# A hybrid decoder step on one core: the opening rebuilt, and 1/rms applied when a product leaves PSUM

## The chip, the cores and the metric

The kernel runs on one core of one Trainium2 chip. A core has five engines that run side by side and meet at semaphores: TensorE (PE, matmuls and, as PEld, the loading of their stationary operand), VectorE (DVE), ScalarE (ACT), GpSimd (POOL) and SyncE (SP, which here only issues transfers). Matmuls read SBUF and write PSUM. The metric is the device time of one execution in microseconds. The kernel before takes 1238.84 us, the median of three runs (1238.34 to 1242.91).

## The reference

One step of a one-layer decoder over 336 rows: 16 learned meta rows, 256 prompt rows and 8 sequences of 8 new rows, each of width 2048, all in float32. Cut to what matters here:

```python
xn = rms_norm(h, norm_w)                      # x * rsqrt(mean(x*x) + eps) * norm_w
proj = xn @ w_in                              # 2048 -> z | x,B,C | dt | z_pool | u | two gates
xbc, conv_new = causal_dwconv(x_B_C, ...)     # 4 taps, then silu
y = ssd(xs, softplus(dt), B, C, state) + xs * d_skip
y = group_norm(y * silu(z)) * ssd_norm_w      # 4 groups of 512 columns
branch_ssd  = y @ w_proj_ssd
pooled = means(u, windows 2, 4, 8, 16) - u
branch_pool = (pooled @ mix + b) * scale * silu(z_pool) @ w_proj_pool
h_new = h + (sigmoid(g1) * branch_ssd + sigmoid(g2) * branch_pool) @ w_out
y_out = rms_norm(h_new, final_norm_w)
```

The norm divides a whole row of x by one number. So 1/rms may be applied to x, or to the product of the unnormed x with a weight, column by column of the transposed product.

## The kernel before, in words

Everything is held transposed: columns of the model on the 128 partitions, the 336 rows (T) along the free axis. x is 16 slices of 128 x 336, kept as four tiles of four slices, its quarters.

A **unit** is one block of 128 output columns: a product over 16 slices, for which a weight tile arrives as two halves of 128 x 1024. Matmuls take operands of type fp32r, so each operand is split into a rounded high part and a low rest, and three products are added: high x high, low x high, high x low. One unit is thus 48 matmuls into one PSUM buffer (`acc`). The weights are split as they come: ScalarE rounds (`prep_hi`, line 144), VectorE subtracts (`prep_lo`, line 150). There are 156 units in a fixed list: 4 B, 4 C, 16 xs, 16 z, then gates, the branch products, pooling and the output.

The order of the work is written out by hand. A unit has four **ticks**, one per quarter of its product. At tick `q` the program emits one step of weight preparation, one quarter of matmuls, and then whatever was put down for that tick with `at(q, ...)` or `later(d, ...)`. Each engine executes its own instructions in that order, so a tick is a place in every queue, not a time. Three halves of weights are prepared ahead of the matmuls; four buffers of each kind (`raw`, `hi`, `lo`) bound how far.

*Opening* (lines 184 to 268). Ten matmuls on ones warm TensorE up. For unit 0, each quarter of x is scaled by `norm_w` and split without its row norm (`wh`, `wl`), and its 12 matmuls follow, with four small ones for dt. Meanwhile GpSimd and ScalarE square x and GpSimd adds the squares. After unit 1 `rstd_make` turns their sum into 1/rms over all 336 rows at once. Units 0 to 7 use `wh`, `wl`; their evacuation multiplies by 1/rms (`raw=True` in `conv`). During them `xnorm` makes a second, normed split of x (`xh`, `xl`) on VectorE, ScalarE and GpSimd, which units 8 and later use; their evacuations from PSUM are ScalarE copies, Silu or Sigmoid.

*SSD stage* (ticks 52 to 152 and a little beyond). The state-space part of four groups, 24 ticks apart, is woven into the xs and z units. In it GpSimd scales the carried states (`hin`, line 624) and masks B (`bm`, line 482), TensorE makes the new states (`ps_hn`, line 630), and VectorE adds them. `z_evac` forms silu(z), multiplies y and squares it; GpSimd adds the four squares of a group (`ss`, line 667); `norm_group` sums them over the partitions with one matmul by ones (`ps_gn`, line 672).

## Time and profile before

| what | value |
|---|---|
| runs | 1238.84 us median, 1238.34 to 1242.91 |
| the profiled execution, its span | 1239.1 us, at a mean granted clock of 0.994 |
| TensorE busy | 1203.4 us (97%), 8066 instructions |
| VectorE, ScalarE, GpSimd busy | 728.4, 557.7, 159.4 us |
| HBM read and written | 186.34 and 15.32 MB |

The profile is one execution. Its views are: groups of equal instructions (busy time in all, mean of one in ns, idle time before them and what ended it), the busy time of each engine by stretch of time, the timeline (start, length, engine, line, operation, output and inputs; the bracket is the idle time before it and what ended that), and lists of who waited for whom. Matmuls are pipelined: the time of one is read from the distance between two starts, not from its own length.

### The profile page before, as it was taken

To read this page: it belongs to the slowest core of one execution; us is meant where nothing else is said; L and a number is where in the kernel's file an instruction comes from. 1 tells how busy PE (TensorE), PEld (TensorE's weight loads), DVE (VectorE), ACT (ScalarE), POOL (GpSimd) and SP (SyncE) were. 2 spreads that over 40 slices of the span, in tenths; PEclk is the share of its full clock that TensorE was granted. 3 is DMA by queue.
4 is the path that set the end of the run, shared out by engine and by line. 5 is a ranking of instruction groups with operands and counts; after the bars stand their busy time and mean duration, and the time that the engine had idled before them with its cause. 6 is when DMAs were issued, how large, how long until landed. Compare 5 with 4: busy or idle time off the path is not lost.

```text
span 1239.1 us, 19826 instructions
## 1 busy us (share of the span) xinstructions
PE 1203.4 (97%) x8066; PEld 1165.4 (94%) x8066; DVE 728.4 (59%) x1008; ACT 557.7 (45%) x792; POOL 159.4 (13%) x161
## 2 busy tenths in 40 slices
PE   6999999999999999999999999999999999999995
PEld 4988988888988999999999999999999999999995
DVE  8798789888887733433445465564343345554543
ACT  4356575748474633333334443434343333334441
POOL 7251142425344000000000000000000000000000
PEclk9999999999999999999999999999999999999998
DMA  5335637475746444444456545554444444456432
GB/s 221 125 125 182 219 126 257 146 243 170 246 143 212 152 156 151 154 153 144 150 161 174 161 150 164 156 156 153 154 153 150 144 149 154 152 170 208 151 120 85
DMA packets 82715, 202.49 MB, mean 163 GB/s; under 512 B 26512, under 2 KB 31280, under 8 KB 82608
## 3 DMA queue, kind: packets, MB, share of 16 engines
q1 hardware_dynamic: 82256, 199.58, 49.9%
q0 software_dynamic: 368, 1.65, 0.4%
q8 instruction: 63, 1.03, 0.3%
q14 instruction: 28, 0.23, 0.1%
HBM read 186.34 MB, written 15.32 MB: 163 GB/s over the span
## 4 chain that ended last, share of the span: by engine, by line
PE 83%; DVE 7%; issue 5%; POOL 3%; ACT 1%; DMA 1%; DVEq 0%; SPq 0%; POOLq 0%; ACTq 0%
PE acc L212 27%; PE acc L213 26%; PE acc L214 26%; DVE lo L150 2%; POOL hin L624 2%; DVE cacc L320 1%; DVE wl L230 1%; DVE x L282 1%; DMA raw<-wall 1%; PE ps_st L565 1%; PE ps_y L579 1%; POOL ss L667 1%; DVE hn L955 0%; POOL bm L482 0%; DVE hin L632 0%
## 5 line engine op out<-in xcount | busy, mean ns | idle before, releaser
L150 DVE TENSOR_TENSOR lo<-raw,hi 128x1024 fp32r<-128x1024 f32 x312 | 392.6, 1260 | 352.6 <-ACT hi L144 352.5
L144 ACT ACTIVATE hi<-raw 128x1024 fp32r<-128x1024 f32 x312 | 329.8, 1058 | 530.5 <-PE acc L213 438.3
L212 PE MATMUL acc<-xh,hi 128*128 128x320 f32 (+4 forms) x1536 | 480.5, 313 | 0.0
L213 PE MATMUL acc<-xl,hi 128*128 128x320 f32 (+4 forms) x1536 | 477.9, 311 | 0.0
L214 PE MATMUL acc<-xh,lo 128*128 128x320 f32 (+4 forms) x1536 | 476.9, 310 | 0.7 <-DVE lo L150 0.7
L212 PEld LDWEIGHTS acc<-xh,hi 128*128 128x128 f32 x1536 | 288.8, 188 | 2.6 <-issue 1.3
L214 PEld LDWEIGHTS acc<-xh,lo 128*128 128x128 f32 x1536 | 288.9, 188 | 1.0 <-DVE lo L150 1.0
L213 PEld LDWEIGHTS acc<-xl,hi 128*128 128x128 f32 x1536 | 288.7, 188 | 1.2
L213 PE MATMUL acc<-pl,hi 128*128 128x320 f32 x256 | 79.4, 310 | 0.0
L214 PE MATMUL acc<-ph,lo 128*128 128x320 f32 x256 | 79.3, 310 | 0.0
L212 PE MATMUL acc<-mh,hi 128*128 128x320 f32 x256 | 79.2, 309 | 0.0
L213 PE MATMUL acc<-ml,hi 128*128 128x320 f32 x256 | 79.1, 309 | 0.0
L214 PE MATMUL acc<-mh,lo 128*128 128x320 f32 x256 | 79.1, 309 | 0.0
L212 PE MATMUL acc<-ph,hi 128*128 128x320 f32 x256 | 79.1, 309 | 0.0
L212 PE MATMUL acc<-yh,hi 128*128 128x320 f32 x256 | 78.7, 308 | 0.0
L213 PE MATMUL acc<-yl,hi 128*128 128x320 f32 x256 | 78.7, 308 | 0.0
L214 PE MATMUL acc<-yh,lo 128*128 128x320 f32 x256 | 78.7, 308 | 0.0
L624 POOL TENSOR_TENSOR hin<-hin,E 128x512 f32<-128x512 f32 x32 | 50.9, 1618 | 52.4 <-ACT E L542 41.9
L320 DVE SCALAR_TENSOR_TENSOR cacc<-rawf,par,cacc 128x360 f32<-128x360 f32 (+1 forms) x72 | 49.1, 682 | 2.1 <-ACT cacc L316 0.4
L212 PEld LDWEIGHTS acc<-ph,hi 128*128 128x128 f32 x256 | 48.4, 189 | 0.0
L213 PE MATMUL acc<-wl,hi 128*128 128x336 f32 (+1 forms) x128 | 43.7, 341 | 4.8 <-DVE wl L230 4.7
L214 PEld LDWEIGHTS acc<-ph,lo 128*128 128x128 f32 x256 | 48.2, 188 | 0.0
(221 smaller groups left out, 1436.8 us busy)
## 6 DMA issues: line engine op xcount, KB each, us to landing
raw<-wall SPq DMA_DIRECT2D x312, 512.0 KB, 3.5
hin<-ssmT SPq DMA_DIRECT2D x16, 512.0 KB, 6.8
ossms<-hin SPq DMA_DIRECT2D x16, 512.0 KB, 5.8
bc<-acT SPq DMA_DIRECT2D x8, 672.0 KB, 6.9
hn<-xT SPq DMA_DIRECT2D x4, 640.0 KB, 6.9
x<-xT SPq DMA_DIRECT2D x3, 672.0 KB, 8.2
opool<-u SPq DMA_DIRECT2D x16, 100.0 KB, 3.1
oconv<-rawf SPq DMA_DIRECT2D x24, 45.5 KB, 4.0
```

What stands on the lines that cost most here:

```text
L144: S.activation(hi, r, AF.Copy)
L150: V.tensor_tensor(out=lo, in0=r, in1=hi.bitcast(F32), op=ALU.subtract)
L212: PE.matmul(acc[:, :n], lhsT=hi[:, c], rhs=bh, start=first, stop=False)
L213: PE.matmul(acc[:, :n], lhsT=hi[:, c], rhs=bl, start=False, stop=False)
L214: PE.matmul(acc[:, :n], lhsT=lo[:, c], rhs=bh, start=False, stop=last)
L230: V.scalar_tensor_tensor(out=wl[q][:, c, :], in0=xg[q][:, c, :], scalar=pc("norm_w", k), in1=wh[q][:, c, :].bitcast(F32), op0=ALU.mult, op ...
L282: V.scalar_tensor_tensor(out=x, in0=x, scalar=pc("norm_w", k), in1=rstd, op0=ALU.mult, op1=ALU.mult)
L320: V.scalar_tensor_tensor(out=a[:, a0:], in0=r[:, a0 + k:k + ACCW], scalar=pc("conv_w", 4 * c + k), in1=a[:, a0:], op0=ALU.mult, op1=ALU.add)
L565: PE.matmul(p, lhsT=st["bt"][:, i, :], rhs=st["xdt"][:, i, :], start=(i == 0), stop=False)
L579: PE.matmul(p[64 * e:64 * e + 64, a:b], lhsT=st["xdt"][:n, i, 64 * hh:64 * hh + 64], rhs=m[:n, e, o:o + b - a], start=(i == 0), stop=(i == ...
L624: GP.tensor_tensor(out=hv, in0=hv, in1=E, op=ALU.mult)
L667: later(1, lambda: GP.tensor_tensor(out=gn[g], in0=gn[g], in1=sq, op=ALU.add))
```

## The change

The opening is written anew, and the second split of x is gone.

- Units 0 and 1 go through the quarters of x together: 24 matmuls per quarter, ordered by part (high x high of both units, low x high, high x low). The half tiles of unit 1 are loaded and split in between. There are 16 warm-up matmuls for 10.
- In the opening GpSimd has no arithmetic and issues no transfers: scaling the dt weights is VectorE's, the squares are ScalarE's, their sums VectorE's (behind the fourth quarter), and `ident`, `sconv`, `umask` and `cmask` are loaded through SP.
- The unnormed split is kept for the whole kernel (its tiles now lie in the long-lived slots). So every evacuation of a product with x multiplies by 1/rms, on VectorE: `conv` always, `u_evac`, and `times_rstd` in `z_evac`, `zp_evac`, `gs_evac`, `gp_evac`, with ScalarE's Silu or Sigmoid one tick later. The copy of the conv history goes from GpSimd to ScalarE.
- `spread_rstd` replaces `rsqrt`, for x and for the four group norms: three matmuls sum over the partitions into a 128 x 3 result, the root is taken on those, VectorE makes three diagonal tiles, and three matmuls by ones spread the result over all partitions.
- The first evacuations come at ticks 14, 16, 18 and so on.

```diff
-NACC, NTR, NWARM = 3, 3, 10
+NACC, NTR, NWARM = 3, 3, 16
...
+    def spread_rstd(ss, n, scale, name, done):
+        at_ = (0, 128, n - 128)
+        p = ps.tile([128, 512], F32, tag="st", name=f"ps_sum{name}")
+        for i, t0 in enumerate(at_):
+            PE.matmul(p[:, i:i + 1], lhsT=ss[:, t0:t0 + 128], rhs=ones[:, 0:1], start=True, stop=True, skip_group_check=True)
...
+        def f1():
+            V.tensor_scalar(out=v, in0=p[:, 0:3], scalar1=scale, scalar2=EPS, op0=ALU.mult, op1=ALU.add)
+            S.activation(t, v, AF.Sqrt)
+        def f2():
+            V.reciprocal(out=r, in_=t)
...
+            for i in range(3):
+                V.tensor_scalar(out=dg[:, i, :], in0=ident, scalar1=r[:, i:i + 1], scalar2=None, op0=ALU.mult)
+        def f3():
+            q = ps.tile([128, 512], F32, tag="st", name=f"ps_rs{name}")
+            for i, t0 in enumerate(at_):
+                PE.matmul(q[:, t0:t0 + 128], lhsT=ones, rhs=dg[:, i, :], start=True, stop=True, skip_group_check=True)
+            later(1, lambda: done(q))
+        later(1, f1)
+        later(2, f2)
+        later(3, f3)
...
+    for q in range(4):
+        h = q // 2
+        if q == 0:
+            prep_hi(0, 0)
+            split_hi(0)
+            prep_hi(1, 0)
+            split_lo(0)
+            prep_lo(0, 0)
+            V.tensor_copy(out=pbs, in_=warm[:, 0:16])
+            prep_lo(1, 0)
+            V.tensor_tensor(out=wdt, in0=wdt, in1=par[:, o:o + 16].unsqueeze(2).to_broadcast([128, KT, NH]), op=ALU.mult)
         else:
+            split_hi(q)
+            if q < 3:
+                prep_hi(q - 1, 1)
+            split_lo(q)
+            if q < 3:
+                prep_lo(q - 1, 1)
+        for part in range(3):
+            for u in range(2):
...
+    prep_hi(2, 0)
+    for q in range(4):
+        S.activation(sq[q], xg[q], AF.Square)
+    prep_hi(2, 1)
+    prep_lo(2, 0)
+    for d, e in ((0, 1), (2, 3), (0, 2)):
+        V.tensor_tensor(out=sq[d], in0=sq[d], in1=sq[e], op=ALU.add)
...
-    def xnorm(k):
-        q, c = divmod(k, 4)
-        x = xg[q][:, c, :]
-        V.scalar_tensor_tensor(out=x, in0=x, scalar=pc("norm_w", k), in1=rstd, op0=ALU.mult, op1=ALU.mult)
...
-        GP.tensor_copy(out=rs[:, :, 0:3], in_=sconv[:, c, :].rearrange("p (b j) -> p b j", b=NSEQ))
+        S.activation(rs[:, :, 0:3], sconv[:, c, :].rearrange("p (b j) -> p b j", b=NSEQ), AF.Copy)
...
-        else:
-            S.activation(r[:, 3 + lo:3 + NP_], acc[:, 0:NP_ - lo], AF.Copy)
-            S.activation(rs[:, :, 3:], v(acc, lo), AF.Copy)
+        V.tensor_tensor(out=r[:, 3 + lo:3 + NP_], in0=acc[:, 0:NP_ - lo], in1=rstd[:, lo:NP_], op=ALU.mult)
+        V.tensor_tensor(out=rs[:, :, 3:], in0=v(acc, lo), in1=v(rstd, 0), op=ALU.mult)
...
+    def times_rstd(t, acc):
+        V.tensor_tensor(out=t, in0=acc[:, 0:TV], in1=rstd[:, NMETA:T], op=ALU.mult)
...
-        S.activation(sz, acc[:, 0:TV], AF.Silu)
+        times_rstd(sz, acc)
         y = xs[g][:, c, NMETA:T]
-        later(1, lambda: V.tensor_tensor(out=y, in0=y, in1=sz, op=ALU.mult))
+        later(1, lambda: S.activation(sz, sz, AF.Silu))
+        later(2, lambda: V.tensor_tensor(out=y, in0=y, in1=sz, op=ALU.mult))
...
-    at(7, rstd_make)
-    at(11, draw_turn)
-    for k in range(KT):
-        at(8 + 5 * k // 4, lambda k=k: xnorm(k))
+    now[0] = 8
+    at(9, rstd_make)
+    at(15, draw_turn)
...
-                at(max(4 * i + 4, 8 + i), lambda i=i, k=kind, j=idx, a=acc: evac(i, k, j, a))
+                at(max(4 * i + 4, 14 + 2 * i), lambda i=i, k=kind, j=idx, a=acc: evac(i, k, j, a))
```

Three places show how instructions move. First TensorE's queue at its start. Before (`acc_138` is unit 0, the numbered `wh`, `wl` the quarters, `hi_0`, `lo_0` the parts of a first half tile):

```order
L204 MATMUL ps_warm<-ones 128x128 x10
L212 MATMUL acc_138<-wh_100,hi_0_139 128x336
L213 MATMUL acc_138<-wl_104,hi_0_139 128x336
L214 MATMUL acc_138<-wh_100,lo_0_141 128x336
L212 MATMUL acc_138<-wh_100,hi_0_139 128x336
```

Now (`acc_153` is unit 0, `acc_154` unit 1; the split of x is called `xh`, `xl`):

```order
L225 MATMUL ps_warm<-ones 128x128 x16
L275 MATMUL acc_153<-xh_101,hi_0_155 128x336 x4
L275 MATMUL acc_154<-xh_101,hi_0_161 128x336 x4
L275 MATMUL acc_153<-xl_105,hi_0_155 128x336 x4
L275 MATMUL acc_154<-xl_105,hi_0_161 128x336 x4
L275 MATMUL acc_153<-xh_101,lo_0_167 128x336 x4
L275 MATMUL acc_154<-xh_101,lo_0_170 128x336 x4
L278 MATMUL ps_dt_152<-x_93,wdt 32x336 x4
```

A slice's low part stood in the second place of the queue; now eight matmuls stand ahead of the first low part of x and sixteen ahead of the first low part of a weight.

Second, GpSimd's queue around the group norm of group 0, in the SSD stage of group 2 (`ss` sums the squares `sqy`, `hin` are the carried states). Before:

```order
L482 TENSOR_TENSOR bm_1_2938<-br_2848,umask 120x640
L667 TENSOR_TENSOR ss_2701<-ss_2701,sqy_3003 128x320
L624 TENSOR_TENSOR hin_0_2811<-hin_0_2811,E_2698 128x512 x2
L667 TENSOR_TENSOR ss_2701<-ss_2701,sqy_3094 128x320
L624 TENSOR_TENSOR hin_1_2813<-hin_1_2813,E_2698 128x512 x2
```

Now, and on to the last add for group 1 (`ss_3104`):

```order
L685 TENSOR_TENSOR ss_2659<-ss_2659,sqy_2983 128x320
L638 TENSOR_TENSOR hin_0_2770<-hin_0_2770,E_2656 128x512 x2
L638 TENSOR_TENSOR hin_1_2772<-hin_1_2772,E_2656 128x512 x2
L685 TENSOR_TENSOR ss_2659<-ss_2659,sqy_3081 128x320
L638 TENSOR_TENSOR hin_2_2831<-hin_2_2831,E_2656 128x512 x2
```

```order
L685 TENSOR_TENSOR ss_3104<-ss_3104,sqy_3415 128x320
L496 TENSOR_TENSOR bm_0_3566<-br_3478,umask 120x512
L496 TENSOR_TENSOR bm_1_3568<-br_3478,umask 120x640
L685 TENSOR_TENSOR ss_3104<-ss_3104,sqy_3528 128x320
L638 TENSOR_TENSOR hin_0_3440<-hin_0_3440,E_3325 128x512 x2
```

The last add of group 0 moved behind two more `hin` products; that of group 1 moved behind the two `bm` products, ahead of which it stood.

Third, TensorE's queue three ticks after group 0's sums (unit 30, `acc_3189`), where before the unit's matmuls followed `ps_hn` at once:

```order
L618 MATMUL ps_yt_0_3206<-ident,yo_0_2887 128x128 x4
L644 MATMUL ps_hn_2_3211<-xr_0_2864,bm_0_2895 128x512
L182 MATMUL ps_rsg_3214<-dgg_3130,ones 128x128 x3
L230 MATMUL acc_3189<-xh_102,hi_0_3039 128x320
L231 MATMUL acc_3189<-xl_106,hi_0_3039 128x320
```

The spread of the group's 1/rms (`ps_rsg`, from the diagonals `dgg`) now stands ahead of the rest of the unit.

More of the change, by code (lines that the diff above doesn't have):

```diff
@@ L110, in hybrid_step @@
     pbs = cp.tile([128, 16], F32, name="pbs")
+    rstd = cp.tile([128, T], F32, name="rstd_x")
     def pc(name, i):
@@ L216, in hybrid_step, with split_hi @@
     psd = ps.tile([128, 512], F32, tag="tr", name="ps_dt0", bufs=NTR)
-    acc0 = ps.tile([128, 512], F32, tag="acc", name="acc0", bufs=NACC)
-    prep(0, 0)
-    for q in range(4):
-        if q == 2:
-            prep(0, 1)
+    acc2 = [ps.tile([128, 512], F32, tag="acc", name=f"acc{j}", bufs=NACC) for j in range(2)]
+    o = _PC["norm_w"][0]
+    def split_hi(q):
         for c in range(4):
@@ L256, in rstd_make, with done @@
     def rstd_make():
-        pst = ps.tile([128, 512], F32, tag="st", name="ps_rms")
-        for q in (0, 2, 3):
-            PE.matmul(pst[:, :T], lhsT=ones, rhs=sq[q][:, 0, :], start=(q == 0), stop=(q == 3))
-        for f in rsqrt(rstd, pst[:, :T], T, "i"):
-            f()
-        V.tensor_tensor(out=draw, in0=psd[:, :T], in1=rstd, op=ALU.mult)
-        drop("sq0", "sq1", "sq2", "sq3")
-        for q in range(4):
-            xh.append(slot(f"xh{q}", [128, 4, T], F32R))
-            xl.append(slot(f"xl{q}", [128, 4, T], F32R))
+        def done(p):
+            S.activation(rstd, p[:, :T], AF.Copy)
+            V.tensor_tensor(out=draw, in0=psd[:, :T], in1=rstd, op=ALU.mult)
+        spread_rstd(ss[:, 0, :], T, 1.0 / D, "x", done)
     def draw_turn():
@@ L295, in hybrid_step, with conv @@
     prompt = lambda a: a[:, 0:NP_]
-    def conv(c, acc, dst, raw=False, lo=0):
+    def conv(c, acc, dst, lo=0):
         r = cv.tile([128, RAWW], F32, tag="rawf", name=f"rawf{c}")
@@ L325, in silu @@
             S.activation(dst[:, NP_:T].rearrange("p (b j) -> p b j", b=NSEQ), samp(a), AF.Silu)
-        if raw:
-            later(1, first)
-        else:
-            first()
-        later(2 if raw else 1, taps)
-        later(3 if raw else 2, silu)
+        later(1, first)
+        later(2, taps)
+        later(3, silu)
     def samp(a):
@@ L667, in square, with scale @@
                 later(1, lambda: GP.tensor_tensor(out=gn[g], in0=gn[g], in1=sq, op=ALU.add))
-            later(2, square)
+            later(3, square)
     def norm_group(g):
-        p = ps.tile([128, 512], F32, tag="st", name=f"ps_gn{g}")
-        PE.matmul(p[:, :TV], lhsT=ones, rhs=gn[g], start=True, stop=True)
-        def scale():
+        def scale(r):
             for c in range(4):
                 y = xs[g][:, c, NMETA:T]
-                V.scalar_tensor_tensor(out=y, in0=y, scalar=pc("ssd_norm_w", 4 * g + c), in1=r, op0=ALU.mult, op1=ALU.mult)
-        r = tp.tile([128, TV], F32, tag="rstd", name=f"rg{g}", bufs=1)
-        f1, f2 = rsqrt(r, p[:, :TV], TV, f"g{g}")
-        later(1, f1)
-        later(2, f2)
-        later(4, scale)
+                V.scalar_tensor_tensor(out=y, in0=y, scalar=pc("ssd_norm_w", 4 * g + c), in1=r[:, :TV], op0=ALU.mult,
+                                       op1=ALU.mult)
+        spread_rstd(gn[g], TV, 1.0 / 512, f"g{g}", scale)
     def y_split(g):
@@ L735, in zp_evac @@
             pool["z", g] = slot(f"zp{g}", [128, 4, TV])
-        S.activation(pool["z", g][:, c, :], acc[:, 0:TV], AF.Silu)
+        t = pool["z", g][:, c, :]
+        times_rstd(t, acc)
+        later(1, lambda: S.activation(t, t, AF.Silu))
     ph, pl_ = {}, {}
@@ L759, in gs_evac @@
         t = extra["t"].tile([128, TV], F32, tag="gs", name=f"gs{m}", bufs=5)
-        S.activation(t, acc[:, 0:TV], AF.Sigmoid)
+        times_rstd(t, acc)
+        later(1, lambda: S.activation(t, t, AF.Sigmoid))
         gates[m] = t
@@ L772, in gp_evac @@
             gpv[q] = slot(f"gp{q}", [128, 4, TV])
-        S.activation(gpv[q][:, c, :], acc[:, 0:TV], AF.Sigmoid)
+        t = gpv[q][:, c, :]
+        times_rstd(t, acc)
+        later(1, lambda: S.activation(t, t, AF.Sigmoid))
     def bp_evac(m, acc):
@@ L914, in hybrid_step @@
         else:
[L915 removed]
+            acc = ps.tile([128, 512], F32, tag="tr" if i == 3 else "acc", name=f"acc{i}", bufs=NACC)
         for qq in range(4):
```

117 lines of the change are left out of this document (50 added, 67 removed).

## The prediction, made before the changed kernel was run

> **What bounds the kernel now.** First the page, then the busy time by stage, then the timeline of the first 100 us, then the waits of the middle. From the page:
>
> ```profile
> span 1239.1 us, 19826 instructions
> L150 DVE TENSOR_TENSOR lo<-raw,hi 128x1024 fp32r<-128x1024 f32 x312 | 392.6, 1260 | 352.6 <-ACT hi L144 352.5
> ```
>
> The view by stage (per stretch: length, then busy us and count of PE, PEld, DVE, ACT, POOL; clock; DMA) tells where TensorE isn't the limit:
>
> ```profile
> 0.00:33.00 33.00, 22.58 (x81) 14.64 (x81) 26.91 (x26) 14.58 (x20) 23.22 (x22) 1.00 0.57 210
> 60.00:100.00 40.00, 37.37 (x243) 35.80 (x242) 39.19 (x57) 23.36 (x41) 19.53 (x21) 1.00 0.48 152
> 170.00:200.00 30.00, 28.52 (x192) 26.73 (x191) 29.41 (x42) 17.34 (x33) 19.50 (x23) 1.00 0.44 131
> 200.00:230.00 30.00, 30.00 (x207) 26.12 (x206) 22.48 (x46) 19.85 (x34) 3.60 (x6) 1.00 0.79 284
> 230.00:260.00 30.00, 27.55 (x186) 25.58 (x186) 29.41 (x45) 18.67 (x34) 18.68 (x19) 1.00 0.42 128
> 290.00:320.00 30.00, 27.79 (x194) 25.91 (x193) 28.36 (x46) 19.88 (x26) 15.80 (x12) 1.00 0.40 123
> 400.00:1200.00 800.00, 800.00 (x5441) 799.84 (x5440) 380.82 (x448) 315.16 (x408) 2.98 (x2) 1.00 0.49 157
> ```
>
> From 400 us on TensorE never waits and VectorE has half its time free: evacuations moved to VectorE cost nothing there, and a microsecond won or lost earlier reaches the end whole. So two places decide: the opening (81 matmuls in 33 us) and the SSD stretches, where VectorE is 95 to 98% busy. The opening's rows (start, us, engine, line):
>
> ```profile
> 1.06 4.64 PE L204 MATMUL ps_warm<-ones 128*128 128x128 f32 x20 [1.06 <-DVE ones L201]
> 5.20 1.06 ACT L144 ACTIVATE hi<-raw 128x1024 fp32r<-128x1024 f32 x1 [3.18 <-DMA raw<-wall]
> 6.89 1.04 ACT L225 ACTIVATE wh<-x,par 128x336 fp32r<-128x336 f32 x2 [0.17 <-DMA x<-xT]
> 7.43 0.39 DVE L227 TENSOR_SCALAR wh<-x,par 128x336 fp32r<-128x336 f32 x1
> 7.86 7.14 DVE L230 SCALAR_TENSOR_TENSOR wl<-x,par,wh 128x336 fp32r<-128x336 f32 x4
> 9.30 5.34 POOL L233 TENSOR_TENSOR sq<-x 128x1344 f32<-128x1344 f32 x2
> 9.53 1.50 ACT L225 ACTIVATE wh<-x,par 128x336 fp32r<-128x336 f32 x3 [1.60 <-DMA x<-xT]
> 12.48 1.50 ACT L225 ACTIVATE wh<-x,par 128x336 fp32r<-128x336 f32 x3 [0.50 <-DMA x<-xT]
> 16.50 1.31 ACT L235 ACTIVATE sq<-x 128x1344 f32<-128x1344 f32 x1
> 27.59 2.01 DVE L230 SCALAR_TENSOR_TENSOR wl<-x,par,wh 128x336 fp32r<-128x336 f32 x4
> 27.70 0.62 PE L212 MATMUL acc<-wh,hi 128*128 128x336 f32 x1 [1.39 <-DVE wh L227]
> 33.60 0.48 PE L214 MATMUL acc<-wh,lo 128*128 128x336 f32 x1
> 33.88 0.37 PE L212 MATMUL acc<-wh,hi 128*128 128x336 f32 x1
> 34.39 0.31 PE L212 MATMUL acc<-wh,hi 128*128 128x336 f32 x1
> 34.54 0.31 PE L213 MATMUL acc<-wl,hi 128*128 128x336 f32 x1
> 15.91 1.35 PE L240 MATMUL ps_dt<-x,wdt 128*32 128x336 f32 x8
> 35.40 0.77 PE L240 MATMUL ps_dt<-x,wdt 128*32 128x336 f32 x8
> 60.49 0.31 PE L212 MATMUL acc<-wh,hi 128*128 128x324 f32 x1
> 92.04 0.31 PE L212 MATMUL acc<-xh,hi 128*128 128x336 f32 x1
> ```
>
> Two things cost time here. Four low splits on VectorE took 7.14 us while GpSimd squared x, and 2.01 us once GpSimd had stopped. And matmuls start 0.28 us apart up to 33.88 and 0.15 us apart behind it (the two pairs of rows): TensorE ran at half speed through the whole opening, though the clock column says 1.00. Unit 4 starts at 60.49 us, unit 8 at 92.04.
>
> **The opening.** Before, one unit waits for each quarter of x; now two do, with no GpSimd arithmetic. Loads: 512 + 672 KB separate the two quarter landings at 9.53 and 12.48, so 0.25 us per 100 KB. By the new order of loads the second quarter comes 256 KB later than before (10.2), the third at 13.8, the fourth at 16.7, unit 2's first half tile at 18.9. ScalarE (1.06 per half tile, 1.50 per quarter, 4 squares of 1.31) ends the fourth quarter at 18.3, the squares at 25.2, unit 2's second tile at 26.3. VectorE, at the undisturbed prices (0.39 + 2.01 per quarter, 1.26 per half tile; the wdt product, half a tile's size, estimated at 0.63): first quarter and two low tiles by 11.1, wdt 11.8, second quarter 14.2, tile, third 17.9, tile, fourth 21.5, unit 2's first low tile 22.8; then the squares' adds (1344 columns estimated at 1.65, so 3 x 1.65 + 0.83 + 0.41, two of them behind the last square) to 29.7, second low tile 31.0.
>
> TensorE at full speed needs 24 x 0.153 + 0.77 = 4.45 us per quarter for both units. It starts at 7.95 (the ScalarE row at 6.89 ends then), waits some 0.6 for the second unit's tile, and is from then on the slowest of the three: quarters end at 13.1, 17.5, 22.0, 26.4. Unit 2's second half comes at 30.1 + 0.7 for the sum matmuls, just as its low tile is ready at 31.0; unit 2 ends at 34.5, unit 3 (with the spread of 1/rms) at 42.5, and with the transposes unit 4 starts at 42.8. That is 17.7 less than 60.49. Half speed is the doubt: 16 warm-up matmuls at 4.64 / 10 each last to 8.5, right up to the work; if they fail, the opening runs at 0.28 until TensorE has been busy long enough, which took 27.70 to 33.9 before; half of 6.2 is 3.1. I take -17.0, bounds -18 to -14.
>
> The Trainium skill, "TensorE: Matmul & The Clock Gate", section "Part 1: The HAM clock gate", says that the array runs at half clock until one busy window of about 3.4 us, and goes back after an idle one. By it the longer warm-up always holds such a window, and the short waits behind it should not undo it: the sum would start from -17.7. The switch at 33.88 agrees with its first half; nothing here shows the second.
>
> Units 4 to 7: VectorE lost 16 products by 1/rms (L282), 39.19 of 40 us were full. The waits between 60 and 100 us (us in total, times, longest):
>
> ```profile
> PE acc L214 <- DVE lo L150: 2.6, 4, 1.0
> ```
>
> The evacuations of units 0 to 4 now come every second tick and VectorE falls some 3 us behind, within the three half tiles that it runs ahead. So -2.6, bounds -2.6 to 0. The constants' loads move from GpSimd's queue to SP, ahead of unit 2's tile; that is in the landings above.
>
> **The SSD stage gives some back.** Rows for the prices (timelines, groups by shape, and waits from 120 to 400 us):
>
> ```profile
> 51.40 0.43 DVE L306 TENSOR_TENSOR rawf<-acc,rstd 128x272 f32<-128x272 f32 x1
> 51.75 0.21 DVE L307 TENSOR_TENSOR rawf<-acc,rstd 128x64 f32<-128x64 f32 x1
> L767 DVE TENSOR_TENSOR m<-acc,gs 128x320 f32<-128x320 f32 x16 | 7.9, 492 | 21.6 <-PE acc L214 21.6
> L166 DVE RECIPROCAL rg<-ntg 128x320 f32<-128x320 f32 x3 | 6.4, 2145 | 0.7 <-ACT ntg L163 0.7
> PE ps_hn L630 <- DVE hin L632: 4.2, 5, 1.1
> PE ps_gn L672 <- POOL ss L667: 4.4, 2, 2.9
> L817 PE MATMUL ps_fin<-ones,fss 128*128 128x1 f32 x6 | 0.7, 236 | 0.0
> 298.26 3.58 POOL L624 TENSOR_TENSOR hin<-hin,E 128x512 f32<-128x512 f32 x2 [10.47 <-PE ps_y L579]
> 303.60 3.34 POOL L624 TENSOR_TENSOR hin<-hin,E 128x512 f32<-128x512 f32 x3
> 341.20 3.23 POOL L482 TENSOR_TENSOR bm<-br,umask 120x512 fp32r<-120x512 f32 x2 [1.56 <-DVE br L486]
> 344.24 0.70 PE L672 MATMUL ps_gn<-ss,ones 128*128 128x320 f32 x2
> ```
>
> Evacuations: VectorE gets 0.43 + 0.21 per xs unit and 0.49 per z unit. Two full stretches hold some 6 xs units (3.9 us), the two later ones some 7 z units (3.4), so at most 7.3 become TensorE waits. Against it: GpSimd's small copies of the conv history are gone, and each group norm loses a 2.15 us reciprocal and three wide operations for narrow ones. At best -0.5; I take +1.5, near the low end, since only the ps_hn waits show VectorE deciding (4.2 us).
>
> GpSimd's order: z now passes VectorE first, so the last add of a group's squares comes a tick later. For group 0 it stands behind four hin products, not two: by 303.60's row two more take 2.2 to 3.6. For group 1 it stands behind the two bm products, which end at 344.4; the add, estimated by its 320 columns against hin's 512 at 0.7 to 1.1, then ends 0.9 to 1.3 after ps_gn's 344.24. TensorE waits in order, with the unit's matmuls behind it. +3.5, bounds 0 (VectorE catches up meanwhile) to 6.
>
> TensorE's own work: a group norm costs 0.7 for three sums and about 0.7 for three spreads, by the L817 row, against 0.70 now (L672): +0.7 or so for each of four, +2.5 taken, 0 to 3. New wait: the spread stands three ticks behind the sums (16 ticks are 31.55 us by the rows of units 4 and 8, so some 6 us), needs a ScalarE root and nine short VectorE operations by then, and holds one of two PSUM buffers that ps_hn also uses; all matmuls queue behind it. +0.5, bounds 0 to 4.
>
> **Sum** from the profiled 1239.1: -17.0 - 2.6 + 1.5 + 3.5 + 2.5 + 0.5 = -11.6, so 1227.5. The runs' median, 1238.84, is 0.3 less: 1227. All best: -21 (1218). All worst: +6 (1245).
>
> **Rivals.** (1) The SSD stage gives nothing back: -17 - 2.6 with at most 0.5 of cost, 1219. For: its waits are 9 us in 260, and a wait in one place lets VectorE catch up for the next. Against: the two GpSimd queues above. (2) It gives back twice as much, 16 us: 1235. For: 29.4 of 30 us busy leaves no room. (3) The opening stays at half speed for long: four quarters of 24 x 0.28 + 1.35 = 8.07 from 7.95 end at 40 and not 26, 1241; with one late switch, 1230. Against: before, about 6 us without a long gap sufficed. The Trainium skill's "TensorE: Matmul & The Clock Gate", Part 1, gives this only if an idle window comes between warm-up and work. (4) Slower: VectorE in the SSD stage has no room at all, and each of the 32 evacuations there becomes a TensorE wait: 16 x 0.64 + 16 x 0.49 = 18.1, with 6 from GpSimd and 3 of norm work 27, against 19.6: 1246. It decides once more than 11 of the 18 show as waits. Against: between the full stretches VectorE is 75% busy (200 to 230).
>
> **How the numbers follow.** Forecast (1222 to 1233) 0.60; (1) 0.16; (2) 0.13; (3) 0.07; (4) 0.04. Range 1218 to 1236: from all best to just beyond (2). Half a per cent, 6.2 us, is about what a measurement here tells from no change: faster means below 1232.6, slower above 1245.0. Faster: nearly all of the forecast and (1), a fifth of (2): 0.78. Slower 0.04, same 0.18.
>
> **What would show it.** Right: first two units done near 26 us with matmuls 0.15 apart and low splits at 0.5 each; unit 4 near 43, unit 8 near 72; no lo waits there; longer ps_sumg waits on GpSimd's ss than 4.4 us; TensorE full from 385 on. Wrong: spacing of 0.28 beyond 13 us, VectorE ending unit 2's tile after 33, or SSD waits on VectorE well over 15 us.

## The result and the profile after

The changed kernel takes 1218.38 us, the median of four runs (1217.66 to 1220.42), against 1239.56 for the kernel before (four runs, 1238.34 to 1242.91): a ratio of 0.983, 95% interval 0.9815 to 0.985. The forecast was 1227 with a range of 1218 to 1236. The direction was right, the gain was under-estimated by 9 us, and the time, 0.4 us inside the range, is that of rival (1), 1219. The profiled execution is the longest of the four. From the page of the changed kernel (low splits: count, busy us, mean ns, idle before them; the span is 1218.6 us):

```profile
L151 DVE TENSOR_TENSOR lo<-raw,hi 128x1024 fp32r<-128x1024 f32 x312 | 387.0, 1241 | 258.9 <-ACT hi L145 258.9
```

The view by stage of the changed kernel (length; busy us and count of PE, PEld, DVE, ACT, POOL; clock; DMA):

```profile
0.00:33.00 33.00, 29.48 (x181) 25.57 (x182) 24.58 (x37) 20.44 (x25) 0.34 (x6) 0.95 0.70 261
60.00:100.00 40.00, 40.00 (x267) 38.73 (x267) 33.25 (x70) 24.15 (x44) 0.30 (x3) 1.00 0.50 158
170.00:200.00 30.00, 30.00 (x200) 27.25 (x199) 27.68 (x55) 16.95 (x31) 3.55 (x7) 1.00 0.87 283
200.00:230.00 30.00, 30.00 (x213) 27.63 (x212) 27.52 (x46) 16.41 (x29) 16.75 (x15) 1.00 0.35 119
230.00:260.00 30.00, 27.93 (x189) 24.70 (x188) 26.45 (x51) 19.33 (x29) 5.03 (x5) 1.00 0.85 280
260.00:290.00 30.00, 27.10 (x180) 24.41 (x179) 22.32 (x44) 16.47 (x25) 21.23 (x19) 0.89 0.42 141
```

TensorE ran 181 matmuls in the first 33 us, not 81, and is full from 60 to 100. VectorE now has 27.5 to 27.7 us of work in both stretches from 170 to 230, where it had 29.4 and 22.5; TensorE waits in neither. The same work lies some 20 us earlier now, so a stretch doesn't hold the same units before and after. Time is lost from 230 to 260, in two waits of 2.1 us together, and above all from 260 to 290, at a clock of 0.89.

Where the time went shows best in when TensorE begins a unit (the first matmul of it in each timeline, us):

| | unit 2 | unit 4 | unit 8 | unit 10 | unit 40 | end |
|---|---|---|---|---|---|---|
| before | 45.07 | 60.49 | 92.04 | 114.29 | 404.16 | 1239.1 |
| changed | 29.66 | 46.19 | 74.48 | 93.44 | 383.04 | 1218.6 |
| gained up to there | 15.4 | 14.3 | 17.6 | 20.9 | 21.1 | 20.5 |

So 14.3 us come from the opening, 3.3 from units 4 to 7, another 3.3 from units 8 and 9, and the SSD stage (units 10 to 39) gives nothing back: 289.9 us before, 289.6 now. The opening of the changed kernel on TensorE and VectorE (start, us; the bracket is the idle time before and what ended it):

```profile
1.06 5.43 PE L225 MATMUL ps_warm<-ones 128*128 128x128 f32 x32 [1.06 <-DVE ones L222]
7.20 0.55 PE L275 MATMUL acc<-xh,hi 128*128 128x336 f32 x2 [0.71 <-DVE xh L244]
8.56 0.89 PE L275 MATMUL acc<-xh,hi 128*128 128x336 f32 x2 [0.82 <-ACT xh L242]
10.33 0.89 PE L275 MATMUL acc<-xh,hi 128*128 128x336 f32 x4 [0.88 <-ACT hi L145]
11.05 2.26 PE L275 MATMUL acc<-xl,hi 128*128 128x336 f32 x8
13.12 2.10 PE L275 MATMUL acc<-xh,lo 128*128 128x336 f32 x8
15.85 1.50 PE L275 MATMUL acc<-xh,hi 128*128 128x336 f32 x8
17.18 1.40 PE L275 MATMUL acc<-xl,hi 128*128 128x336 f32 x8
...
12.88 2.01 DVE L248 SCALAR_TENSOR_TENSOR xl<-x,par,xh 128x336 fp32r<-128x336 f32 x4
```

Four low splits take 2.01 us, as forecast. The first quarter waits three times, 2.4 us in all, and then eight matmuls take 2.26 and 2.10 us where eight take 1.40 a little later: half speed again, from 11.25 to 14.66 us in the trace's record of the granted clock, which changes only in steps of 3.41 us. From 15.85 on a quarter takes 4.6 us.

In the SSD stage the waits of the changed kernel are (us in all, times, longest), and its rows around 281 us:

```profile
PE ps_sumg L163 <- POOL ss L685: 3.2, 2, 2.9
PE ps_hn L644 <- DVE hin L646: 2.1, 2, 1.0
```

```profile
272.64 7.32 POOL L638 TENSOR_TENSOR hin<-hin,E 128x512 f32<-128x512 f32 x4 [4.52 <-ACT E L556]
279.93 1.10 POOL L685 TENSOR_TENSOR ss<-ss,sqy 128x320 f32<-128x320 f32 x1
...
281.08 1.44 PE L163 MATMUL ps_sumg<-ones,ss 128*128 128x1 f32 x6 [2.90 <-POOL ss L685]
284.85 0.47 PE L230 MATMUL acc<-xh,hi 128*128 128x320 f32 x1
285.11 0.47 PE L231 MATMUL acc<-xl,hi 128*128 128x320 f32 x1
...
287.91 0.31 PE L230 MATMUL acc<-xh,hi 128*128 128x320 f32 x1
```

This is the predicted queue: group 0's last add stood behind four `hin` products. What was not predicted is behind it: 0.26 between matmuls (284.85 and 285.11) and, from 287.7 on, 0.15. The array went to half speed for 6.83 us, from 280.90 on by the clock record.

### The profile page after: what moved, and what is told of

Read it like the earlier page. It is cut to its first block, busy times and chain, and to the rows that moved or that the text cites. A ratio compares the mean times of both kernels' runs of the same rounds, so it can differ in the third digit from the quotient of the medians.

```text
span 1218.6 us, 19976 instructions
## 1 busy us (share of the span) xinstructions
PE 1197.0 (98%) x8124; PEld 1169.4 (96%) x8124; DVE 739.4 (61%) x1141; ACT 540.1 (44%) x735; POOL 105.2 (9%) x107
## 4 chain that ended last, share of the span: by engine, by line
PE 85%; DVE 6%; DMA 4%; issue 2%; ACT 1%; POOL 1%; SPq 0%; DVEq 0%; POOLq 0%
PE acc L231 27%; PE acc L230 27%; PE acc L232 27%; DMA bc<-acT 3%; DVE lo L151 2%; PE acc L275 1%; DVE cacc L337 1%; DMA raw<-wall 1%; DVE M L547 1%; DVE hin L646 1%; DVE hn L969 0%; DMA ossms<-hin 0%; POOL hin L638 0%; PE ps_y L593 0%; PE ps_hn L644 0%
## 5 line engine op out<-in xcount | busy, mean ns | idle before, releaser
L151 DVE TENSOR_TENSOR lo<-raw,hi 128x1024 fp32r<-128x1024 f32 x312 | 387.0, 1241 | 258.9 <-ACT hi L145 258.9
L230 PE MATMUL acc<-xh,hi 128*128 128x320 f32 (+4 forms) x1632 | 511.2, 313 | 0.0
L231 PE MATMUL acc<-xl,hi 128*128 128x320 f32 (+4 forms) x1632 | 508.5, 312 | 0.0
L232 PE MATMUL acc<-xh,lo 128*128 128x320 f32 (+4 forms) x1632 | 507.2, 311 | 0.0
L230 PEld LDWEIGHTS acc<-xh,hi 128*128 128x128 f32 x1632 | 307.4, 188 | 2.5 <-issue 0.8
L231 PEld LDWEIGHTS acc<-xl,hi 128*128 128x128 f32 x1632 | 307.3, 188 | 1.1
L232 PEld LDWEIGHTS acc<-xh,lo 128*128 128x128 f32 x1632 | 307.6, 188 | 0.0
L231 PEld LDWEIGHTS acc<-ml,hi 128*128 128x128 f32 x256 | 48.1, 188 | 0.0
L230 PEld LDWEIGHTS acc<-mh,hi 128*128 128x128 f32 x256 | 48.1, 188 | 0.0
L231 PEld LDWEIGHTS acc<-pl,hi 128*128 128x128 f32 x256 | 48.1, 188 | 0.0
```

Source lines behind the costliest of these rows:

```text
L151: V.tensor_tensor(out=lo, in0=r, in1=hi.bitcast(F32), op=ALU.subtract)
L230: PE.matmul(acc[:, :n], lhsT=hi[:, c], rhs=bh, start=first, stop=False)
L231: PE.matmul(acc[:, :n], lhsT=hi[:, c], rhs=bl, start=False, stop=False)
L232: PE.matmul(acc[:, :n], lhsT=lo[:, c], rhs=bh, start=False, stop=last)
```

## The experiments

The theory at the start: (a) the opening gained by taking GpSimd's squares from beside VectorE and by giving TensorE enough work to stay warm; (b) units 4 to 7 gained since VectorE lost 16 products; (c) the SSD stage gave nothing back since VectorE works ahead there. All kernels are the changed kernel with one edit (later_fill has two of them together). Each row is one execution. The times are read by stretch, as in the table above, since the edits are far apart. Units 10 to 40 took 287.9 to 291.9 us in the seven kernels whose edits leave that stage alone (changed, the four open kernels and the two xnorm kernels), so a difference inside these 4 us shows nothing:

| kernel | unit 2 | unit 2 to 8 | unit 8 to 10 | unit 10 to 40 | span |
|---|---|---|---|---|---|
| changed | 29.66 | 44.8 | 19.0 | 289.6 | 1218.6 |
| open_gp | 32.41 | 44.8 | 19.0 | 290.9 | 1222.7 |
| open_single | 29.08 | 44.7 | 19.0 | 287.9 | 1216.3 |
| open_fill | 32.31 | 44.8 | 19.0 | 290.3 | 1221.3 |
| open_fill3 | 27.74 | 44.8 | 19.0 | 289.0 | 1216.1 |
| xnorm_dve | 27.08 | 44.8 | 21.1 | 288.5 | 1217.1 |
| xnorm_both | 27.42 | 47.5 | 27.6 | 291.9 | 1230.1 |
| evac_x2 | 27.92 | 44.8 | 19.0 | 296.0 | 1223.3 |
| ss_dve | 27.50 | 45.0 | 19.0 | 287.4 | 1214.5 |
| norm_later | 27.76 | 44.8 | 19.0 | 284.3 | 1211.0 |
| lo_late | 27.26 | 44.8 | 19.0 | 290.4 | 1240.1 |
| later_fill | 27.97 | 44.8 | 19.0 | 289.9 | 1216.9 |

### GpSimd's squares back in the opening

```diff
+        if q < 2:
+            GP.tensor_tensor(out=sq[q], in0=xg[q], in1=xg[q], op=ALU.mult)
         for part in range(3):
...
-    for q in range(4):
+    for q in range(2, 4):
         S.activation(sq[q], xg[q], AF.Square)
```

> The changed kernel with the squares of the first two quarters of x on GpSimd again, beside the splits (two instructions, 5.34 us in the kernel before). Theory: GpSimd's squares stretch what VectorE does beside them (four low splits 7.14 us for 2.01), so the first two quarters' splits end 3 to 4 us later and unit 2 starts at 32 to 33.5 instead of 29.66; the end is 2 to 4 us later. Rival: the long splits of before came from waits for ScalarE and the loads: low splits stay at 0.5 each and unit 2 starts within 0.5 us of 29.66, or earlier, as ScalarE has two squares less.

The timeline of this kernel, VectorE and GpSimd:

```profile
6.58 6.38 DVE L248 SCALAR_TENSOR_TENSOR xl<-x,par,xh 128x336 fp32r<-128x336 f32 x4
...
16.25 2.01 DVE L248 SCALAR_TENSOR_TENSOR xl<-x,par,xh 128x336 fp32r<-128x336 f32 x4
...
7.04 2.43 POOL L270 TENSOR_TENSOR sq<-x 128x1344 f32<-128x1344 f32 x1 [6.59 <-DMA x<-xT]
10.13 2.46 POOL L270 TENSOR_TENSOR sq<-x 128x1344 f32<-128x1344 f32 x1 [0.66 <-DMA x<-xT]
```

The theory holds. The four splits took 6.38 us, 4.4 more than undisturbed, against 4.9 us of GpSimd's work: VectorE got almost nothing done while GpSimd ran. Unit 2 starts 2.8 us later than in the changed kernel's profile, and 4.5 to 5.3 later than in six other executions of the same opening (xnorm_dve, xnorm_both, evac_x2, ss_dve, norm_later, lo_late: 27.08 to 27.92). Not all of that is VectorE's stretching: behind the longer waits TensorE was at half speed from 12.21 to 19.04 us by the clock record, about 3.4 us lost.

The Trainium skill, "SBUF — State Buffer", section "Who interferes with whom", says that a VectorE instruction with two SBUF inputs contends with a GpSimd instruction that reads SBUF, through a lock held for the whole instruction, and that one with at most one SBUF input, outside VectorE's two-port modes, doesn't. The 4.4 of 4.9 us agree with a lock.

### One unit through the quarters instead of two

```diff
-halves = [(0, 0), (1, 0), (0, 1), (1, 1)] + [(i, h) for i in range(2, NU) for h in range(2)]
+halves = [(i, h) for i in range(NU) for h in range(2)]
...
-            for u in range(2):
+            for u in range(1):
...
+    for part in range(3):
+        for k in range(16):
+            PE.matmul(acc2[1][:, :T], lhsT=whl[1, k // 8][part // 2][:, 128 * (k % 8):128 * (k % 8) + 128],
+                      rhs=(wl if part == 1 else wh)[k // 4][:, k % 4, :], start=(k == 0 and part == 0), stop=(k == 15 and part == 2))
```

The loads and splits are put in the order that this needs: all quarters of x come ahead of unit 1's half tiles.

> The changed kernel with only unit 0 going through the quarters of x, and unit 1 behind it whole; still no GpSimd arithmetic. Theory: two units to a quarter matter, because one unit's 2.6 us of matmuls per quarter are less than the 3.5 us between two quarters, so TensorE waits about 1 us in each, stays at half speed (0.28 between matmuls) and unit 2 starts at 32 to 34. Rival: taking GpSimd out was all: unit 2 starts at 28 to 30, the end is the same.

The timeline of open_single, TensorE:

```profile
12.85 1.21 PE L275 MATMUL acc<-xl,hi 128*128 128x336 f32 x4
16.02 1.52 PE L275 MATMUL acc<-xl,hi 128*128 128x336 f32 x4
...
26.60 2.64 PE L282 MATMUL acc<-xh,lo 128*128 128x336 f32 x16
29.08 0.32 PE L229 MATMUL acc<-xh,hi 128*128 128x336 f32 x1
```

The rival is nearer. TensorE follows VectorE in the second and third quarter (four matmuls in 1.21 and 1.52 us, not 0.78), but the array stays at full speed, and unit 2 starts at 29.08: 1.2 to 2.0 us later than the shared opening in the six executions named above. The quarters arrive and are split fast enough without GpSimd, so sharing is worth at most 2 of the opening's 14 to 17 us.

### Filling the waits of the first quarter

Nine small matmuls on ones, ahead of the three matmuls that waited.

```diff
+                    if (q, part) == (0, 0) and (u, c) in ((0, 0), (0, 2), (1, 0)):
+                        for j in range(FILL[u, c]):
+                            PE.matmul(warm[:, 128:256], lhsT=ones, rhs=ones, start=True, stop=True, skip_group_check=True)
```

> The changed kernel with nine more small matmuls on ones (three ahead of unit 0's first, third and unit 1's first high matmul of the first quarter), where TensorE waited 0.71, 0.82 and 0.88 us. Theory: these waits between 7.2 and 10.3 us sent the array back to half speed from 11.25 to 14.67 us. With them filled the two groups of eight that took 2.26 and 2.10 us take 1.4 each, the clock shows no step back, unit 2 starts near 28.1 instead of 29.66 and the end is 1.5 us earlier. Rival: the step back comes at its time whatever TensorE does then: unit 2 at 29.6 to 30, the same end.

This was built badly: the filling matmuls wrote the warm-up's PSUM buffer, so the first of them waited 2.85 us for VectorE's copy of it (`pbs`), and unit 2 started at 32.31. It says nothing on either theory. In open_fill2 and open_fill3 they write a buffer of their own (`fill`).

> As open_fill, but the nine small matmuls (two, three and four in the three places, 0.22 us each at full speed) write a PSUM buffer of their own, so none waits for the copy of the warm-up's result on VectorE, which cost open_fill 2.85 us. Theory: with the waits of the first quarter filled, the array is not sent back to half speed; unit 2 starts at 27.0 to 28.1, as in xnorm_dve, whose waits were shorter (27.08), against 29.66. Rival: the step back does not hang on these waits; a stretch at half speed shows between 8 and 16 us again and unit 2 starts at 29 or later.

> The kernel of open_fill2 once more, since in that execution every matmul of the run took several times as long as in any other. Expectations are the same: unit 2 starts at 27.0 to 28.1 us and no half-speed stretch shows after the warm-up, by the theory that the waits of the first quarter cause it; by the rival such a stretch shows again and unit 2 starts at 29 or later.

The timeline of open_fill3, TensorE:

```profile
8.89 1.05 PE L279 MATMUL fill<-ones 128*128 128x128 f32 x8
9.93 0.89 PE L280 MATMUL acc<-xh,hi 128*128 128x336 f32 x4
10.66 1.40 PE L280 MATMUL acc<-xl,hi 128*128 128x336 f32 x8
11.89 1.39 PE L280 MATMUL acc<-xh,lo 128*128 128x336 f32 x8
```

In open_fill2 the whole execution took 5432 us, a matmul some 1.0 us long instead of 0.3, so its times are not used. In open_fill3 no matmul of the opening waits, none runs at half speed, and unit 2 starts at 27.74, as the theory said. But six executions without any filling also stayed at full speed (27.08 to 27.92); they waited 0.9 to 1.8 us there, the changed kernel's profile 2.4. So the step back is an accident of that execution, worth 1.7 to 2.6 us, and filling only guards against it. That the longer waits cause it agrees with all of these; that filling prevents it was not shown, since the kernel without filling mostly stays fast too.

### The second split's work put back, without a reader

```diff
+    def xnorm(k):
+        q, c = divmod(k, 4)
+        x = xg[q][:, c, :]
+        V.scalar_tensor_tensor(out=x, in0=x, scalar=pc("norm_w", k), in1=rstd, op0=ALU.mult, op1=ALU.mult)
+        later(1, lambda: S.activation(sq[q][:, c, :], x, AF.Copy))
+        later(2, lambda: GP.tensor_tensor(out=sq[q][:, c, :], in0=x, in1=sq[q][:, c, :], op=ALU.subtract))
+    for k in range(KT):
+        at(14 + k, lambda k=k: xnorm(k))
```

xnorm_dve has it without the two `later` lines, xnorm_both with them.

> The changed kernel with the 16 products of x by 1/rms put back on VectorE, one per tick from 14 to 29, with no reader (the work of ScalarE and GpSimd on the second split stays out). Theory: VectorE's own load made the waits for low tiles of units 4 to 7: 16 products of about 0.57 us are 9.1 us, VectorE runs 6 to 9 us ahead there now, so the waits come back in part, 1 to 3 us, and unit 8 starts at 75.5 to 77.5 instead of 74.48. Rival: the products alone fit into the lead, and it was GpSimd's subtractions beside them that made VectorE late: unit 8 within 0.5 us of 74.48.

> As xnorm_dve (16 products on VectorE, ticks 14 to 29), with the copies on ScalarE and the subtractions on GpSimd behind them too: all of the second split's work, with no reader. xnorm_dve lost nothing in units 4 to 7 (44.81 us against 44.82) and 2.2 in units 8 and 9 (21.15 against 18.96). Theory now: GpSimd's subtractions beside VectorE made it late; units 4 to 7 take 46 to 48 us from unit 2 to unit 8, low tiles are waited for, and units 8 and 9 lose 2 to 4. Rival: before, the lead was lost to the late opening; here unit 2 to unit 8 stays within 0.5 of 44.8.

Groups of VectorE from 40 to 100 us (count, busy us, mean ns), first of xnorm_dve:

```profile
L337 DVE SCALAR_TENSOR_TENSOR cacc<-rawf,par,cacc 128x360 f32<-128x360 f32 (+1 forms) x30 | 17.5, 585 | 0.7
L883 DVE SCALAR_TENSOR_TENSOR x<-x,par,rstd_x 128x336 f32<-128x336 f32 x15 | 7.9, 561 | 0.0
```

and of xnorm_both, with its waits from 26 to 100 us:

```profile
L337 DVE SCALAR_TENSOR_TENSOR cacc<-rawf,par,cacc 128x360 f32<-128x360 f32 (+1 forms) x27 | 19.4, 717 | 0.6
L883 DVE SCALAR_TENSOR_TENSOR x<-x,par,rstd_x 128x336 f32<-128x336 f32 x15 | 13.5, 931 | 0.0
```

```profile
PE acc L232 <- DVE lo L151: 3.8, 4, 1.7
PE ps_cum L391 <- DVE dtw L382: 2.9, 1, 2.9
```

The products alone cost nothing in units 4 to 7 (the rival of the first run): some 8 us more of VectorE's time went into its lead. From 60 to 100 us the shortest time between the end of a half tile's low split and the matmul that needs it fell from 5.7 to 1.2 us. With GpSimd's subtractions beside them each product took 931 ns instead of 561, each tap of the convolution 717 instead of 585, and the low tiles were waited for again: units 2 to 7 took 2.7 us longer, the theory of the second run. So the gain of units 4 to 7 belongs to GpSimd's subtractions as much as to the products. The copies on ScalarE came back with the subtractions, and no run has one without the other. Units 8 and 9 lost 8.7 us, more than the 2 to 4 expected: the chain that makes dt on VectorE came late, TensorE waited 2.9 us for it, and the array was at half speed from 94.64 to 101.47.

### The evacuations of the SSD stage done twice

```diff
-        V.tensor_tensor(out=r[:, 3 + lo:3 + NP_], in0=acc[:, 0:NP_ - lo], in1=rstd[:, lo:NP_], op=ALU.mult)
-        V.tensor_tensor(out=rs[:, :, 3:], in0=v(acc, lo), in1=v(rstd, 0), op=ALU.mult)
+        for _ in range(1 + (1 if c < 16 else 0)):
+            V.tensor_tensor(out=r[:, 3 + lo:3 + NP_], in0=acc[:, 0:NP_ - lo], in1=rstd[:, lo:NP_], op=ALU.mult)
+            V.tensor_tensor(out=rs[:, :, 3:], in0=v(acc, lo), in1=v(rstd, 0), op=ALU.mult)
...
-        times_rstd(sz, acc)
+        for _ in range(2):
+            times_rstd(sz, acc)
```

> The changed kernel with the products by 1/rms of the 16 xs and 16 z evacuations done twice on VectorE (16 x 0.64 + 16 x 0.49 = 18.1 us more of VectorE's time in the SSD stage; results the same). Theory (VectorE works ahead): low tiles are ready 3.2 to 13 us before TensorE takes them, and a stretch of 30 us gets 2 to 3 us more, so this costs 0 to 2 us. Rival (each evacuation is a TensorE wait, the predicted price's upper end): 11 to 18 us more; a price between, as I had forecast it for the first 18 us, would be 1.5.

The waits of evac_x2 in the SSD stage (us in all, times, longest):

```profile
PE ps_hn L645 <- DVE hin L647: 6.6, 6, 1.7
PE ps_sumg L163 <- POOL ss L687: 3.9, 1, 3.9
```

Neither number came. Units 10 to 40 take 296.0 us, 6.4 more than in the changed kernel: above 0 to 2, below 11 to 18. No low tile was waited for, though the lead was used up in one place (0.05 us at 224 us); the waits are for the `hin` adds (6.6 for 2.1 us), which have no lead, since TensorE can make the next `ps_hn` only when the add has emptied a PSUM buffer. So a second 18 us of evacuations did not fit into VectorE's free time, and cost about a third of their price.

The first 18 us seem to have cost nothing, but no run takes them out again, and VectorE's work did not grow by all of it. A row of the changed kernel, whole execution (count, busy us, mean ns):

```profile
L172 DVE RECIPROCAL srg<-srg 128x3 f32<-128x3 f32 x4 | 0.7, 170 | 0.6 <-ACT srg L169 0.6
```

In units 10 to 39 the evacuations of xs and z add 16.9 us. But the reciprocal of a group norm, 2145 ns before (L166), takes 170 now: the norm's steps on 128 x 320, 14.5 us there, became steps on 128 x 3 and three diagonals, 6.2 us. That gives about half back. All instructions of VectorE in those units took 268.9 us for 259.4.

### The sum of squares on VectorE

```diff
-                later(1, lambda: GP.tensor_tensor(out=gn[g], in0=gn[g], in1=sq, op=ALU.add))
+                later(1, lambda: V.tensor_tensor(out=gn[g], in0=gn[g], in1=sq, op=ALU.add))
```

> The changed kernel with the adds of a group's squares on VectorE instead of GpSimd (12 instructions, 128x320). Theory: group 0's last add stood behind four hin products of 1.83 us on GpSimd, TensorE waited 2.90 us for it at 281 and was then at half speed for 6.83 us; VectorE runs 4 to 6 us ahead there and has no such queue. The wait and the half-speed stretch go: units 29 takes about 10.5 us instead of 15.5, the end is 4 to 6 us earlier. Rival: the add only moves to another late queue: VectorE's low tiles or the squares on ScalarE come later, TensorE waits as long; or the wait goes but the half speed stays (-2.9 alone).

The waits of ss_dve in the SSD stage:

```profile
PE ps_hn L644 <- DVE hin L646: 3.1, 4, 1.1
PE ps_sumg L163 <- DVE ss L685: 1.2, 1, 1.2
PE ps_rsg L182 <- DVE dgg L177: 0.6, 1, 0.6
```

The half-speed stretch went and the long wait with it, but VectorE's own queue gave several short ones: unit 29 to 30 fell from 15.5 to 11.6 us, units 10 to 40 only from 289.6 to 287.4. That is about half of the expected gain, and 287.4 is hardly outside what the unedited stage takes (287.9 to 291.9); the gain in unit 29 is clear of it, since that unit took 14.9 to 17.4 us in those kernels.

### The group norms two ticks later

```diff
-        at(4 * first["z", 4 * g + 3] + 9, lambda g=g: norm_group(g))
+        at(4 * first["z", 4 * g + 3] + 11, lambda g=g: norm_group(g))
...
-            gn[g] = tp.tile([128, TV], F32, tag="ss", name=f"ss{g}", bufs=1)
+            gn[g] = tp.tile([128, TV], F32, tag="ss", name=f"ss{g}", bufs=2)
```

> The changed kernel with each group norm begun two ticks later (about 4 us), and two buffers for the sum of squares; all else and all prices the same. Theory: at 281 us TensorE waited only because its sums stood too early against GpSimd's queue, and the 2.9 us of idleness sent it to half speed for 6.83 us. Both go: from unit 29 to unit 30 about 10.7 us instead of 15.5, units 10 to 40 about 285 instead of 289.6, end 4 to 5 us earlier than with the same opening. Rival: the half speed in 280.9 to 287.7 has another cause, the many small or narrow matmuls there: the wait goes (-2.9), the step back stays.

The waits of norm_later in the SSD stage:

```profile
PE ps_hn L644 <- DVE hin L646: 1.4, 2, 1.1
PE ps_rsg L182 <- DVE hin L646: 1.3, 1, 1.3
```

Wait and half speed both went: unit 29 to 30 took 9.4 us, units 10 to 40 284.3, 5.3 less than in the changed kernel. The matmuls of that stretch took 281.3 us in all (distances between starts, waits left out) against 284.3, which puts the half speed at 3.0 us and the waits at 2.3 (one of 1.3 us, for the spread, took the place of the long one).

### Low splits behind the tick's other work

```diff
-                if n < len(halves):
-                    prep_lo(*halves[n])
-                load_to(n + 5)
             quarter_mm(i, qq, acc, kind, idx)
...
             tick(4 * i + qq)
+            if qq % 2:
+                if n < len(halves):
+                    prep_lo(*halves[n])
+                load_to(n + 5)
```

> The changed kernel with each low split and the load behind it issued after the tick's other work instead of ahead of it. Theory: in the SSD stage VectorE is not too slow, it does low splits 3 to 13 us before they are needed while an add to hin, which frees the PSUM buffer that ps_hn waits for, stands behind one. With the order turned the two waits for hin (1.02 and 1.05 us at 233 and 236) go or fall below 0.5 in all, and no low tile is waited for; units 10 to 40 take 1.5 to 2.1 less. Rival: VectorE has no room there in any order: the waits stay, or turn into waits for low tiles.

The waits of lo_late for `hin` up to 390 us, then its waits from 400 to 900 us, then a row of VectorE's timeline:

```profile
PE ps_hn L644 <- DVE hin L646: 2.4, 2, 1.8
```

```profile
PE acc L232 <- DVE lo L151: 15.0, 8, 3.7
```

```profile
749.17 0.63 DVE L732 TENSOR_TENSOR ps<-u 128x447 f32<-128x447 f32 x1 [5.02 <-DMA u<-spool]
```

The rival was right in the SSD stage (290.4 us; the waits stayed), so it was not a low split alone that made those adds late; three taps of the convolution (1.85 us) stand ahead of one of them in both kernels. What would free VectorE there stays open. And the edit cost 23 us behind unit 40, where nothing was expected: 15 us of waits in the pooling units, and some 7 us lost in three stretches at half speed behind them (13.7 us by the clock record). VectorE now waits there for a load of the pooling state (`u`) with the low splits queued behind that wait. Up to now they stood ahead of it.

### Both together

> norm_later and open_fill3 together: the group norms two ticks later, and the nine filling matmuls of the first quarter. norm_later took 284.3 us from unit 10 to unit 40 against 289.6, and an opening without a step back ends 1.7 to 2.6 us before that of the changed kernel's profile. Theory: both add up, unit 2 near 27.7, the end at 1211 to 1213, 0.978 of the kernel before, and faster than the changed kernel (0.983). Rival: the 5.3 us of norm_later were luck of one execution with a wait that varies (2.9 to 4.8 us over the runs so far): 1215 to 1218.

1217.14 us, the median of five runs (1213.7 to 1218.67): 0.981 of the kernel before, interval 0.9792 to 0.9826, which overlaps the changed kernel's. So it isn't shown to be faster, and the time lies in the rival's range. Unit 29 took 9.4 us here as in norm_later, so that gain came a second time; it was lost again later. Two rows of its profiled execution, VectorE and TensorE, show where:

```profile
322.60 1.37 DVE L552 TENSOR_SCALAR M<-bc,acum 128x256 f32<-128x256 f32 x6 [4.54 <-DMA bc<-acT]
...
332.78 1.62 PE L183 MATMUL ps_rsg<-dgg,ones 128*128 128x128 f32 x6 [2.71 <-DVE dgg L178]
```

VectorE waited 4.54 us for a load (`bc`); the diagonals of group 1's norm stood behind it, TensorE waited 2.71 us for the spread, and the array was at half speed from 332.11 to 338.93. Unit 34 to 39 took 50.1 us, in norm_later 44.3. The spread of 5 us over the five runs fits this wait coming or not, but only one of them was profiled. Two ticks later removes one wait and puts the norm where a late load can reach it.

## Why the prediction was right, and where its sizes were wrong

**The opening, -17.0: measured -14.3, mechanism right.** The low splits took 2.01 us per four, and GpSimd's squares were shown to be what stretched them (open_gp). Full speed would have had unit 4 at 42.8; it came at 46.19. Of these 3.4 us the first quarter holds 2.75 (15.85 for 13.1): three waits of 2.4 us where 0.6 was counted and 1.6 of half speed behind them, less 0.75 for an earlier start. The rest is 4.6 us per quarter for 4.45. In the six executions that kept their speed unit 4 started at 43.6 to 44.5, -16 to -17 by the sum's way of counting. So the bounds of -18 to -14 held. What I gave as the cause in part, two units to a quarter, is at most 2 us of it (open_single).

The warm-up's 16 matmuls kept the array warm up to the work, but not through it. The Trainium skill, "TensorE: Matmul & The Clock Gate", section "Part 1: The HAM clock gate", was cited with an idle window of about 3.4 us sending the array back, and I wrote that the short waits should not undo it. Half speed followed them all the same: the two waits that lay inside one step of the clock record, 7.84 to 11.25 us, were 1.6 us together. The six other executions, with at most 1.2 us inside a step, kept full speed.

**Units 4 to 7, -2.6: measured -3.3.** Right in size. The step "VectorE lost 16 products" was only half of it: the products alone fit (xnorm_dve), GpSimd's subtractions beside them, with ScalarE's copies, did the rest (xnorm_both).

**Units 8 and 9: not in the sum, -3.3.** The kernel before waits there too (0.7 for a low tile, 0.4 for the dt chain) and then runs at half speed for 3.4 us; its rows from 100 to 120 us have clocks of 0.95 and 0.88, which I did not read. VectorE's earlier arrival removed all of it; the two xnorm runs brought it back.

**Evacuations on VectorE, +1.5: about 0 by the waits.** The step that failed is the reading of a VectorE busy for 29.4 us of 30 as the engine that decides there. In the trace of the kernel before, a half tile's low split ended 3.6 to 13 us before the matmul that needs it, throughout the full stretches (each split's end against the first matmul on it, in order); in the changed kernel it is 3.2 to 16 us. A full VectorE was working ahead, and the narrower norm gave half of the new work back. What has no lead is the `hin` add; TensorE's waits for it went down, 4.2 to 2.1 us, and up to 6.6 only with 18 us more of load (evac_x2). Rival (4), 18 us for the first 32 evacuations, has its price refuted by the same run: a third of it, and only on top of what the change adds.

**GpSimd's order, +3.5: the waits fell by 1.2.** Group 0: 2.90 us for 1.55, right in place, but 1.35 more and not 2.2 to 3.6. Group 1: 0.33 for nothing, forecast 0.9 to 1.3. Not seen: a wait of 2.87 us of the kernel before at group 2, the larger of the two in the quoted row, is gone. There the order of the queue's end is the same, but GpSimd's `hin` products start 4.4 us sooner within the unit and take 3.6 us less (12.8 for 16.4), so the last add ends 5.4 us ahead of the sums; why they are sooner and shorter was not tried. And behind group 0's wait the half speed, +3.0 (norm_later), which no term had.

**TensorE's own norm work, +2.5: measured +2.6** at full speed: for three norms, sums 1.76 and spreads 1.86 us in norm_later, for 1.92 of the one sum before (+1.7); for the fourth, behind unit 40, 1.17 for 0.30.

**The spread's wait, +0.5: 0 in the changed kernel**, but single waits of 1.3 to 2.7 us once the norm was moved. The risk was real, its place was not the one measured first.

In sum the SSD stage was forecast at +8.0 and came out at -0.3, or +0.3 with the 0.6 us lost behind unit 40: waits 9.1 to 5.3 us, matmul time 280.8 to 284.3, which holds 3.0 of half speed. That, and the 3.3 us of units 8 and 9, outweigh the opening's shortfall and make up the 9 us. So the mechanisms of the opening and of units 4 to 7 were right in the main, and the SSD stage's price was not. That the time kept within the range, by 0.4 us, is partly luck: the opening's shortfall of 2.7 us made up for most of the 3.3 us that no term had. That it fits rival (1) so closely is luck too. Its sum has neither the 3.3 us nor the half speed, and of its reason, that a wait lets VectorE catch up for the next, the runs show another form: low tiles lay ready long before they were needed. Of the signs named beforehand two failed outright: the waits for GpSimd's `ss` were 3.2 us and not over 4.4, and matmuls stood 0.28 apart until 14.5 us, beyond 13.

## What to carry to other kernels

Before a busy engine is called full, measure for each of its products how long it lies ready before it is used: an engine that works ahead fills its time and costs nothing until the product without a lead comes late. GpSimd arithmetic beside VectorE instructions that read two SBUF tiles was paid for almost twice (4.4 us of VectorE's time for 4.9 of GpSimd's), so look for it first in any stretch where VectorE sets the pace. And a TensorE wait of 2 to 3 us was worth up to twice its length here (2.9 us, and 3.0 more), since the matmuls behind it ran at half speed.
